# A list scheduler's cost model: transfers with shared rates and margins, and one more accumulating load

## The chip, the cores and the metric

The kernel runs on one core of one Trainium2 chip. The metric is the device time of one execution in microseconds (us). In this document PE is TensorE (matrix products; PEld is its loading of weights), DVE is VectorE, ACT is ScalarE, POOL is GpSimd and SP is SyncE. A load is a DMA transfer from the chip's main memory (HBM) into the on-chip buffer; an accumulating load adds what it brings to what lies there. Both run on 16 DMA engines; the plain ones are issued by SP, the accumulating ones by POOL.

## The reference

A decoder of two layers on 256 positions of width 1024, all in float32:

```python
for i in range(DEPTH):                      # two layers
    if i % 2 == 0:                          # layer 0: spatial gating in 12 groups
        h = x @ a_w_in[li]; u, v, q_mem = split(h)
        mix = gmlp_mixer(u, v, ...)
    else:                                   # layer 1: causal attention, 12 heads of 64
        h = x @ b_w_in[li]; q, k, v, q_mem = split(h)
        mix = moba_attention(q, k, v)       # 256 positions are one block: own block alone
    mem_out = memory_cross_attention(q_mem, mem, w_mem_kv[i])   # 4 heads, 256 memory tokens
    sub = concatenate([mix, mem_out]) @ w_mix_out[i]
    x = layer_norm(ALPHA * x + sub, ...)
    x = layer_norm(ALPHA * x + swiglu(x, w_ffn_in[i], w_ffn_out[i]), ...)

def swiglu(x, w_in, w_out):
    g, u = split(x @ w_in)                  # 1024 -> 2 x 2816
    return (silu(g) * u) @ w_out            # 2816 -> 1024
```

## The kernel before

**Products.** To keep float32 precision on the fast matmul path, every operand is split into a high and a low half (`split`: ACT copies the high half, DVE subtracts it to get the low one), and each product is three passes: high·high, high·low, low·high. So every weight that is loaded costs ACT and DVE a split; 1024 columns of it are one piece.

**Channel mixer.** Its 11 chunks of 256 channels are done as one plain chunk (`R`) and five pairs (`S`, chunks 1-2, 3-4, 5-6, 7-8, 9-10; `PLANS`). A pair computes a 2 x 2 block product with seven instead of eight block products, M1 to M7 (Strassen's way, in `product`). `OPERAND` names the weight blocks of each: M1 needs block 11, M5 needs 11 + 12, M2 needs 21, M6 needs 11 + 22, M3 needs 22, M7 needs 12 + 22, M4 needs 21 + 11, where a former sum stays in its buffer and is part of the next operand. The sums are made in three ways: by DVE (`raw_s<-raw_s,raw_s`), by an accumulating load out of main memory (`LOADED`, M7: `raw_s<-in_w` on POOL) or by an accumulating transfer between two buffers (`MOVED`, M4: `raw_s<-raw_s` on POOL). The results are gathered in X, Y and Z (PSUM tiles), from which ACT and DVE make m1 and m5; `sg` is the silu that m5 needs. PE transposes m1 and m5 (`tp`), the pieces are split again (`ht`), and the output products (`fo`) follow. A last letter f or g in a tile's name stands for layer 0 or 1. In layer 1's first pair the seven products are interleaved with the plain chunk and the second half of the LayerNorm, so that they come in the order M1, M2, M5, M6, M3, M7, M4 (`ffn_steps`).

**Order.** Nothing runs where it is written: `Plan` records all instructions of the program with their dependences and then orders them. TensorE keeps the order of the recording. For DVE, ACT, POOL and SP, `simulate` is a list scheduler: it steps through time with assumed costs (`Op.cost`: `hold` is how long an engine is taken, `lat` when the result can be used), gives each engine the instruction that can start first and, among those, the one that is due first (`late`, from `deadlines`), and keeps an engine free for a short while if a more urgent instruction is about to be ready. Instructions made with `either` (copies and scalings) go to ACT or DVE, whichever is chosen first. It also chooses the slot of each tile. Five sets of constants are tried (`TRIALS`), and the order with the least planned waiting of TensorE is issued. The engines then run in that order, each instruction waiting for its semaphores, so only the order and the slots come from the plan, not the times. Since ACT, DVE, POOL and SP run in order, one that waits holds up all that stand behind it.

**Transfers in the plan before.** One serial link:

```python
size = op.bytes * (2.1 if e == "gpsimd" else 1) / 437
link = max(link, t + 2300) + size
end = max(link, t + 7800 if e == "gpsimd" else 0) + 100
```

Weights come in units of 1 MB (128 x 2048) into six `raw` buffers (`RAW_BUFS`), and ten split pieces (`HALF_BUFS`) are kept. `Stream.make` makes the next piece: it loads ahead as far as buffers are free, forms the sum where there is one, and splits.

Of the kernel before, what the change touches and what calls it, by code (L numbers as in the profile page):

```python
# [46 lines left out]
OPERAND = {"M1": ("11", None), "M5": ("11", "12"), "M2": ("21", None), "M3": ("22", None),  # L47
           "M6": ("11", "22"), "M7": ("12", "22"), "M4": ("21", "11")}
LOADED = ("M7",)
MOVED = ("M4",)  # L50
TAGS = {"11": "gb", "21": "vbig"}

# [150 lines left out]
class Op:  # L203
# [13 lines left out]
    def cost(self):  # L217

        w = max([v.width() for v in self.writes + self.reads] or [1])
        e, n = self.engine, self.name  # L220
        if n == "dma_start":
            v = (self.writes or self.reads)[0]
            self.bytes = 4 * v.ap.ap[0][1] * v.width()
            self.hold, self.lat = (900 if e == "gpsimd" else 400), 0
        elif e == "tensor":
            w = self.args[2].width() if n == "matmul" else P
            f32 = n == "matmul" and self.args[2].root.dtype == F32
            self.hold = max(104, (w + 32) / 2.4) if not f32 else 0.85 * w
            self.lat = 200 + 0.37 * w if not f32 else self.hold + 270
        elif e == "vector":  # L230
            slow = n in ("tensor_scalar_mul", "tensor_scalar_add") or n == "tensor_copy"
            self.lat = 225 + 0.48 * w if n == "tensor_scalar_mul" and w > 8 else 150 + 1.042 * w
            self.hold = self.lat - 82
        elif e == "scalar":
            self.lat = 190 + 0.842 * w + (200 if "accum_out" in self.kw else 0)
            self.hold = self.lat - 100
        else:
            self.lat = self.hold = 700 + 2.5 * w if w < 8 else 250 + 2.0 * w


class Plan:
# [48 lines left out]
    def delay(self, a, b):  # L290

        if a.engine == b.engine and a.name != "dma_start":
            return a.hold
        if a.name == "dma_start":
            return 2300 + a.bytes / 400 if a.engine != "gpsimd" else 2300 + a.bytes / 180
        return a.lat + (50 if b.engine == "tensor" else 33)

    def deadlines(self):
        t = 4300
        for op in self.ops:  # L300
            if op.engine == "tensor":
                op.late = t
                t += op.hold
        for op in self.ops:
            for o in op.before.values():
                o.after.append(op)
        slots, last, follow = {}, {}, {}
        for op in self.ops:
            for b in op.roots:
                last[b] = op.n  # L310
        for op in self.ops:
            for b in op.roots:
                if b.tile is None and b.slot is None:
                    free = slots.setdefault(b.tag, [(0, i, None) for i in range(b.bufs)])
                    free.sort()
                    n, b.slot, was = free.pop(0)
                    if was:
                        follow[was] = op
            for b in op.roots:
                if last[b] == op.n and b.tile is None:  # L320
                    slots[b.tag].append((op.n, b.slot, b))
        for op in reversed(self.ops):
            late = [o.late - self.delay(op, o) for o in op.after if o.late is not None]
            late += [follow[b].late - self.delay(op, follow[b]) for b in op.roots if b in follow]
            if op.late is not None:
                late.append(op.late)
            op.late = min(late) if late else t
            if op.engine == "tensor":
                op.due = op.late

    def order(self):
        self.deadlines()
        best = None
        for trial in self.TRIALS:
            for op in self.ops:
                for b in op.roots:
                    b.slot, b.last, b.left = None, 0.0, 0
            for op in self.ops:
                for b in op.roots:
                    b.left += 1  # L340
            out, lost = self.simulate(*trial)
            self.trials.append(lost)
            if best is None or lost < best[0]:
                best = lost, [(op, op.opens, op.call, op.start, op.end, [b.slot for b in op.opens]) for op in out]
        for op, op.opens, op.call, op.start, op.end, slots in best[1]:
            for b, b.slot in zip(op.opens, slots):
                pass
        return [x[0] for x in best[1]]

    def simulate(self, slip, idle, margin):  # L350
# [2 lines left out]
        head = {e: 0 for e in by_late}  # L353
        gone = set()
        free = {e: 0.0 for e in self.ENGINES}
        busy = dict(free)
        waiting = {op.n: len(op.before) for op in self.ops}
        at = {op.n: 0.0 for op in self.ops}
        ready = {e: [] for e in self.ENGINES}
        tags = {}  # L360
        for op in self.ops:
            for b in op.roots:
                if b.tile is None:
                    t = tags.setdefault(b.tag, {"queue": [], "slots": [(0.0, i) for i in range(b.bufs)]})
                    if b not in t["queue"]:
                        t["queue"].append(b)
        pe = [op for op in self.ops if op.engine == "tensor"]
        ip = 0
        link = 0.0
        for op in self.ops:  # L370
            if not waiting[op.n]:
                for e in op.calls():
                    ready[e].append(op)
        out = []

        def opening(op):

            t0 = at[op.n]
            for b in op.roots:
                if b.slot is not None or b.tile is not None:  # L380
                    continue
                t = tags[b.tag]
                i = t["queue"].index(b)
                need = i + 1 if len(t["slots"]) > i else 0
                if not need:
                    return None
                fit = [x for x in t["slots"] if not b.whole or x[1] in whole]
                if not fit:
                    return None
                t0 = max(t0, min(fit)[0])  # L390
            return t0

        def hope(op, memo, depth):

            if op in memo:
                return memo[op]
            t = at[op.n]
            if waiting[op.n]:
                for o in op.before.values():
                    if o in gone:  # L400
                        continue
                    if o.engine == "tensor":
                        s = free["tensor"] + o.due - pe[ip].due
                    elif depth == 0 or o.name == "dma_start":
                        t = 1e12
                        break
                    else:
                        s = max(hope(o, memo, depth - 1), free[o.engine])
                    t = max(t, s + self.delay(o, op))
            memo[op] = t  # L410
            return t

        while len(out) < len(self.ops):
# [64 lines left out]
            for b in op.opens:  # L478
                q = tags[b.tag]
                q["queue"].remove(b)  # L480
                fit = [x for x in q["slots"] if x[0] <= t] if not b.whole else [x for x in q["slots"] if x[1] in whole]
                s = min([x for x in fit if x[1] not in whole] or fit) if b.psum else min(q["slots"])
                q["slots"].remove(s)
                b.slot = s[1]
            if e == "tensor" and (op.name == "transpose" or op.kw["start"]):
# [2 lines left out]
                if b.tag == "mm":  # L488
                    (whole.add if full else whole.discard)(b.slot)
            if op.name == "dma_start":  # L490
                size = op.bytes * (2.1 if e == "gpsimd" else 1) / 437
                link = max(link, t + 2300) + size
                end = max(link, t + 7800 if e == "gpsimd" else 0) + 100
            else:
                end = t + op.call.lat
            op.end = end
            out.append(op)
            for o in op.after:
                w = t + op.call.hold if o.engine == e and not o.other and op.name != "dma_start" else end + (50 if o.engine == "tensor" else 33)
                at[o.n] = max(at[o.n], w)  # L500
                waiting[o.n] -= 1
                if not waiting[o.n] and o.engine != "tensor":
                    for e2 in o.calls():
                        ready[e2].append(o)
            for b in op.roots:
                b.left -= 1
                b.last = max(b.last, end + 33)
                if not b.left and b.slot is not None:
                    tags[b.tag]["slots"].append((b.last, b.slot))
        return out, lost  # L510

    def emit(self):
# [10 lines left out]
class Stream:  # L523
# [17 lines left out]
    def parts(self, key):  # L541

        if len(key) == 2:
            return [key[0]]
        return [f"{key[0]}_{q}" for q in OPERAND[key[1]][:1 if key[1] in LOADED else 2] if q]

    def unit_ap(self, name):
        off, n = OFFS[name]
# [20 lines left out]
    def make(self):  # L569
# [9 lines left out]
            self.nc.gpsimd.dma_start(self.raw[parts[0]], self.raw[parts[1]], accum_op=ALU.add)  # L579
        elif len(parts) == 2 and key[-1] == 0:  # L580
            self.nc.vector.tensor_add(self.raw[parts[0]], self.raw[parts[0]], self.raw[parts[1]])
        if key[1] in LOADED and key[-1] == 0:
            a, b = (f"{key[0]}_{q}" for q in OPERAND[key[1]])
            self.nc.gpsimd.dma_start(self.raw[a], self.unit_ap(b), accum_op=ALU.add)
        hl = self.tile("spl", [P, 2, 1024], F32R, "spl", "spl_" + "_".join(map(str, key)), HALF_BUFS)
# [875 lines left out]
```

## Time and profile before

| | |
|---|---|
| median of 3 runs | 571.65 us (571.44 to 573.89) |
| the profiled execution | 569.85 us, span from first to last instruction 568.1 us |
| mean granted TensorE clock | 0.992 |
| busy: PE / PEld / DVE / ACT / POOL | 550.0 / 475.2 / 506.1 / 370.8 / 32.7 us |
| moved by DMA | 131.48 MB, mean 231 GB/s |
| issues of 1 MB loads into `raw_s` by SP, median to landing | 40, 7.6 us |
| accumulating loads (`raw_s<-in_w`) / transfers (`raw_s<-raw_s`) by POOL | 10 of each, 9.0 / 7.7 us |

The profile is one execution. A row of the timeline gives the start in us from the span's start, the length, the engine, the line, the operation, the tiles (output<-inputs), the shapes and the count, and in brackets how long the engine was idle before it and whose result ended that. All recorded instructions are issued at line 520, so they are told apart by the names of their tiles. A row of the stretches' table gives each engine's busy time with its number of instructions, in the order PE, PEld, DVE, ACT, POOL, then the granted clock, the busy share of the DMA engines, and GB/s.

### The profile page before, as it was taken

The numbers are of one execution on the slowest core, as the hardware profiler recorded it, in microseconds if no ns is written. First come the engines' busy times: TensorE is split into PE (matmuls) and PEld (weight loads), VectorE is DVE, ScalarE is ACT, GpSimd is POOL, SyncE is SP. The second block draws the span as 40 slices with busy tenths as digits, with TensorE's granted clock in tenths as the row PEclk, the third lists the DMA queues.
The fourth block names the chain that finished last, engine by engine and source line by source line (L and its number), as shares of the span: only waits on it lengthen the run. The fifth ranks groups of instructions, "written<-read, shape, count | busy, mean of one in ns | idle before, by whom it ended". The sixth has DMA issues, their size and how long they took to land. (4 is left out here: it accounts for less than half of the span.)

```text
span 568.1 us, 8070 instructions
## 1 busy us (share of the span) xinstructions
PE 550.0 (97%) x3028; PEld 475.2 (84%) x3028; DVE 506.1 (89%) x674; ACT 370.8 (65%) x563; POOL 32.7 (6%) x44
## 2 busy tenths in 40 slices
PE   8999999999999999999999999999989899999995
PEld 8999879878887888788899989888868688788884
DVE  5789989999989999996987898699999799899965
ACT  6767755696558594774476989566766575848710
POOL 2020000000000000100100000000000000001001
PEclk9999999999999999999999999999999999999998
DMA  8999744576796989799456253352777969797902
GB/s 293 381 379 387 301 177 154 144 213 203 197 377 167 377 215 364 205 346 352 167 186 260 74 186 149 77 172 85 236 219 198 356 171 374 177 359 214 288 1 75
DMA packets 23352, 131.48 MB, mean 231 GB/s; under 512 B 2576, under 2 KB 6288, under 8 KB 9360
## 3 DMA queue, kind: packets, MB, share of 16 engines
q1 hardware_dynamic: 20000, 109.45, 49.7%
q0 software_dynamic: 2880, 20.97, 19.6%
q8 instruction: 24, 0.39, 0.3%
q10 hardware_dynamic: 432, 0.52, 0.3%
q14 instruction: 16, 0.13, 0.1%
HBM read 119.41 MB, written 1.05 MB: 212 GB/s over the span
## 5 line engine op out<-in xcount | busy, mean ns | idle before, releaser
L520 ACT CAST spl_s_M<-raw_s 128x1024 fp32r<-128x1024 f32 x140 | 139.8, 1050 | 53.4 <-DMA raw_s<-in_w 25.1
L520 DVE TENSOR_TENSOR spl_s_M<-raw_s,spl_s_M 128x1024 fp32r<-128x1024 f32 x140 | 164.4, 1219 | 7.2 <-ACT spl_s_M L520 7.0
L520 PE MATMUL fog<-spl_w,htg 128*128 128x512 f32 (+1 forms) x282 | 64.9, 382 | 0.0
L520 PE MATMUL fof<-spl_w,htf 128*128 128x512 f32 x264 | 63.9, 392 | 0.0
L520 ACT CAST spl_w<-raw_w 128x1024 fp32r<-128x1024 f32 x44 | 45.7, 1052 | 27.0 <-DMA raw_w<-in_w 16.0
L520 PEld LDWEIGHTS fog<-spl_w,htg 128*128 128x128 f32 x282 | 51.0, 191 | 9.7
L520 PEld LDWEIGHTS fof<-spl_w,htf 128*128 128x128 f32 x264 | 49.0, 188 | 9.9
L520 DVE TENSOR_TENSOR spl_w<-raw_w,spl_w 128x1024 fp32r<-128x1024 f32 x44 | 53.2, 1218 | 0.4 <-ACT spl_w L520 0.4
L520 DVE TENSOR_TENSOR raw_s<-raw_s,raw_s 128x2048 f32<-128x2048 f32 x20 | 45.7, 2284 | 0.0
L520 PE MATMUL qk<-x2T,spl_qk 128*128 128x256 f32 x288 | 36.4, 284 | 1.2 <-DVE mix L520 1.2
L520 PEld LDWEIGHTS qk<-x2T,spl_qk 128*128 128x128 f32 x288 | 35.2, 192 | 1.4 <-DVE mix L520 1.4
L520 PE MATMUL Xf<-spl_s_M,x1T 128*128 128x512 f32 x120 | 28.4, 391 | 1.3 <-DVE m5f L520 1.2
L520 PE MATMUL Zg<-spl_s_M,SgM 128*128 128x512 f32 x120 | 29.0, 390 | 0.6 <-DVE htg L520 0.6
L520 PE MATMUL Zf<-spl_s_M,SfM 128*128 128x512 f32 x120 | 29.0, 390 | 0.0
L520 PE MATMUL Xg<-spl_s_M,SgM 128*128 128x512 f32 x120 | 29.0, 390 | 0.0
L520 PE MATMUL Xf<-spl_s_M,SfM 128*128 128x512 f32 x120 | 28.8, 389 | 0.0
L520 PE MATMUL Xg<-spl_s_M,x3T 128*128 128x512 f32 x120 | 28.4, 391 | 0.0
L520 PEld LDWEIGHTS Xf<-spl_s_M,x1T 128*128 128x128 f32 x120 | 22.4, 188 | 6.7 <-ACT spl_s_M L520 1.6
L520 PEld LDWEIGHTS Zg<-spl_s_M,SgM 128*128 128x128 f32 x120 | 22.5, 188 | 5.7 <-DVE htg L520 1.1
L520 PEld LDWEIGHTS Xg<-spl_s_M,x3T 128*128 128x128 f32 x120 | 22.4, 188 | 5.1 <-DVE m5g L520 0.3
L520 PEld LDWEIGHTS Xf<-spl_s_M,SfM 128*128 128x128 f32 x120 | 22.5, 188 | 4.7
L520 PEld LDWEIGHTS Xg<-spl_s_M,SgM 128*128 128x128 f32 x120 | 22.5, 188 | 4.6
(245 smaller groups left out, 1004.8 us busy)
## 6 DMA issues: line engine op xcount, KB each, us to landing
raw_s<-in_w SPq DMA_DIRECT2D x40, 1024.0 KB, 7.6
raw_w<-in_w SPq DMA_DIRECT2D x22, 1024.0 KB, 8.6
raw_s<-in_w POOLq DMA_DIRECT2D x10, 1024.0 KB, 9.0
raw_s<-raw_s POOLq DMA_DIRECT2D x10, 1024.0 KB, 7.7
raw_o<-in_w SPq DMA_DIRECT2D x8, 1024.0 KB, 6.3
raw_qk<-in_w SPq DMA_DIRECT2D x6, 1024.0 KB, 4.8
raw_u<-in_w SPq DMA_DIRECT2D x3, 1024.0 KB, 10.1
raw_bv<-in_w SPq DMA_DIRECT2D x4, 768.0 KB, 8.8
```

The lines of the kernel that those rows point to most:

```text
L520: getattr(getattr(self.nc, c.engine), c.name)(*map(real, c.args), **{k: real(v) for k, v in c.kw.items()})
```

## The change

Nothing in what is computed changes, and TensorE's order stays. Two things do.

The first is what the planner believes. `Op.cost` has new figures (a DVE operation on three operands 57 ns more, ACT's accumulating read shared out otherwise, POOL's short operations 985 ns, issues of DMAs 450 and 1000 ns instead of 400 and 900). A result used by the same engine is now ready after its latency, not after the engine's hold; POOL is taken to see a result 500 ns late. Transfers are modelled by a new class, `Wire`, with a queue for plain and one for accumulating transfers, a rate for each, lower rates when both run, at most eight of SP's transfers under way, and a margin (`SPARE`) behind the modelled end before data or a slot count as usable (`sure`).

The second is an operand: in layer 1's first pair (`s1_1`), M5's sum 11 + 12 is formed by an accumulating load of block 12 out of main memory, as M7's already was, and no longer by DVE. Block 12 is still loaded by itself too, for M7.

```diff
+FIRST_LOADED = {"s1_1": ("M5", "M7")}
...
-            self.hold, self.lat = (900 if e == "gpsimd" else 400), 0
+            self.hold, self.lat = (1000 if e == "gpsimd" else 450), 0
...
-            self.lat = 225 + 0.48 * w if n == "tensor_scalar_mul" and w > 8 else 150 + 1.042 * w
+            self.lat = 225 + 0.48 * w if fast else 152 + 1.042 * w
+            if n == "scalar_tensor_tensor" and not psum:
+                self.lat += 57
...
-            self.lat = 190 + 0.842 * w + (200 if "accum_out" in self.kw else 0)
-            self.hold = self.lat - 100
+            self.lat = 190 + 0.842 * w + (90 if "accum_out" in self.kw else 0) - (35 if psum else 0)
+            self.hold = self.lat - 98 + (100 if "accum_out" in self.kw else 0)
...
-            self.lat = self.hold = 700 + 2.5 * w if w < 8 else 250 + 2.0 * w
+            self.lat = self.hold = 985 if w < 8 else 300 + 1.4 * w
+
+class Wire:
+    HARD, SOFT, BOTH, LANES = ((7000, 250), (30000, 370), (1e12, 428)), 223, (155, 123), 8
+    SPARE = 1200, 1800
+
+    def __init__(self):
+        self.now, self.hard, self.soft, self.sent = 0.0, [], [], []
+
+    def lane(self):
+        return self.sent[-self.LANES].end + 30 if len(self.sent) >= self.LANES else 0.0
+
+    def issue(self, op, t):
+        self.run(t, [self.hard, self.soft])
+        if op.engine == "sync":
+            self.sent.append(op)
+        (self.soft if op.engine == "gpsimd" else self.hard).append([op, t + 2350, op.bytes])
+        self.run(1e12, [[list(x) for x in q] for q in (self.hard, self.soft)])
+
+    def run(self, until, queues):
+        hard, soft = queues
+        now = self.now
+        while (hard or soft) and now < until:
+            live = [bool(q) and q[0][1] <= now for q in queues]
+            edge, hard_rate = next(x for x in self.HARD if now < x[0])
+            rates = self.BOTH if all(live) else (hard_rate * live[0], self.SOFT * live[1])
+            ends = [now + q[0][2] / r for q, r, a in zip(queues, rates, live) if a]
+            stop = min(ends + [edge] + [q[0][1] for q, a in zip(queues, live) if q and not a] + [until])
+            for q, r, a in zip(queues, rates, live):
+                if a:
+                    q[0][2] -= (stop - now) * r
+                    if q[0][2] < 1:
+                        op = q.pop(0)[0]
+                        op.end = stop + 100
+                        op.sure = stop + (self.SPARE[op.engine == "gpsimd"] if stop > 20000 else 200)
+            now = stop
+        if until < 1e12:
+            self.now = until
...
-            return a.hold
+            return a.hold if a.engine == "tensor" else a.lat + 35
...
-        return a.lat + (50 if b.engine == "tensor" else 33)
+        return a.lat + {"tensor": 56, "gpsimd": 500}.get(b.engine, 35)
...
+        free["sync"] = 800.0
...
+        def free_at(x):
+            b = x[0]
+            return max([b.last] + [o.sure for o in b.moves]) if b else 0.0
...
-            t0 = at[op.n]
+            t0 = max([at[op.n]] + [o.sure for o in op.moves])
+            if op.engine == "sync":
+                t0 = max(t0, wire.lane())
...
-                t0 = max(t0, min(fit)[0])
+                t0 = max(t0, min(map(free_at, fit)))
...
-                size = op.bytes * (2.1 if e == "gpsimd" else 1) / 437
-                link = max(link, t + 2300) + size
-                end = max(link, t + 7800 if e == "gpsimd" else 0) + 100
+                wire.issue(op, t)
+                end = 0
...
-        return [f"{key[0]}_{q}" for q in OPERAND[key[1]][:1 if key[1] in LOADED else 2] if q]
+        return [f"{key[0]}_{q}" for q in OPERAND[key[1]][:1 if key[1] in FIRST_LOADED.get(key[0], LOADED) else 2] if q]
...
-        if key[1] in LOADED and key[-1] == 0:
+        if key[1] in FIRST_LOADED.get(key[0], LOADED) and key[-1] == 0:
```

More of the change, by code (lines that the diff above doesn't have):

```diff
@@ L220, in cost @@
         e, n = self.engine, self.name
+        psum = any(v.root.psum for v in self.writes + self.reads)
         if n == "dma_start":
@@ L228, in cost @@
             self.hold = max(104, (w + 32) / 2.4) if not f32 else 0.85 * w
-            self.lat = 200 + 0.37 * w if not f32 else self.hold + 270
+            self.lat = (205 + 0.36 * w if n == "matmul" else 273) if not f32 else self.hold + 280
         elif e == "vector":
-            slow = n in ("tensor_scalar_mul", "tensor_scalar_add") or n == "tensor_copy"
-            self.lat = 225 + 0.48 * w if n == "tensor_scalar_mul" and w > 8 else 150 + 1.042 * w
+            fast = n == "tensor_scalar_mul" and w > 8
@@ L304, in deadlines @@
         for op in self.ops:
+            op.moves = [o for o in op.before.values() if o.name == "dma_start"]
             for o in op.before.values():
@@ L336, in order @@
                 for b in op.roots:
-                    b.slot, b.last, b.left = None, 0.0, 0
+                    b.slot, b.last, b.left, b.moves = None, 0.0, 0, []
             for op in self.ops:
@@ L363, in simulate @@
                 if b.tile is None:
-                    t = tags.setdefault(b.tag, {"queue": [], "slots": [(0.0, i) for i in range(b.bufs)]})
+                    t = tags.setdefault(b.tag, {"queue": [], "slots": [(None, i) for i in range(b.bufs)]})
                     if b not in t["queue"]:
@@ L368, in simulate @@
         ip = 0
-        link = 0.0
+        wire = Wire()
         for op in self.ops:
@@ L396, in hope @@
                 return memo[op]
-            t = at[op.n]
+            t = max([at[op.n]] + [o.sure for o in op.moves if o in gone])
             if waiting[op.n]:
@@ L480, in simulate @@
                 q["queue"].remove(b)
-                fit = [x for x in q["slots"] if x[0] <= t] if not b.whole else [x for x in q["slots"] if x[1] in whole]
-                s = min([x for x in fit if x[1] not in whole] or fit) if b.psum else min(q["slots"])
+                fit = [(free_at(x), x[1], x) for x in q["slots"] if not b.whole or x[1] in whole]
+                if b.psum:
+                    fit = [x for x in fit if x[0] <= t and x[1] not in whole] or fit
+                s = min(fit, key=lambda x: x[:2])[2]
                 q["slots"].remove(s)
@@ L490, in simulate @@
             if op.name == "dma_start":
-                size = op.bytes * (2.1 if e == "gpsimd" else 1) / 437
-                link = max(link, t + 2300) + size
-                end = max(link, t + 7800 if e == "gpsimd" else 0) + 100
-            else:
-                end = t + op.call.lat
-            op.end = end
+                wire.issue(op, t)
+                end = 0
+            else:
+                op.end = end = t + op.call.lat
             out.append(op)
             for o in op.after:
-                w = t + op.call.hold if o.engine == e and not o.other and op.name != "dma_start" else end + (50 if o.engine == "tensor" else 33)
-                at[o.n] = max(at[o.n], w)
+                if op.name != "dma_start":
+                    same = o.engine == e == "tensor"
+                    at[o.n] = max(at[o.n], t + op.call.hold if same else end + {"tensor": 56, "gpsimd": 500}.get(o.engine, 35))
                 waiting[o.n] -= 1
@@ L506, in simulate @@
                 b.left -= 1
-                b.last = max(b.last, end + 33)
+                b.last = max(b.last, end + 35)
+                if op.name == "dma_start":
+                    b.moves.append(op)
                 if not b.left and b.slot is not None:
-                    tags[b.tag]["slots"].append((b.last, b.slot))
+                    tags[b.tag]["slots"].append((b, b.slot))
         return out, lost
```

## The prediction

> **What bounds the kernel now.** I read the busy shares first, then the idle time of TensorE in the timeline, because TensorE is busy nearly throughout and only its waits can be won.
>
> ```profile
> PE 550.0 (97%) x3028; PEld 475.2 (84%) x3028; DVE 506.1 (89%) x674; ACT 370.8 (65%) x563; POOL 32.7 (6%) x44
> ```
>
> The TensorE order is written by hand and does not change, so the first instruction after a wait names the wait. These are the timeline's rows of PE with a wait over 0.25 us behind the start phase (start, length, instruction, wait in brackets; the rows between them are left out), and the products that run just before the longest wait (445.83):
>
> ```profile
> 116.68 0.88 PE L520 MATMUL tpf<-ident,hf 128*128 128x128 f32 x4 [1.19 <-DVE hf L520]
> 171.78 0.33 PE L520 MATMUL tpf<-ident,m5f 128*128 128x128 f32 x1 [1.48 <-DVE m5f L520]
> 229.69 2.55 PE L520 MATMUL Xf<-spl_s_M,x1T 128*128 128x512 f32 x10 [1.19 <-DVE m5f L520]
> 336.14 2.06 PE L520 MATMUL qk<-x2T,spl_qk 128*128 128x256 f32 x15 [1.23 <-DVE mix L520]
> 418.87 0.33 PE L520 MATMUL tpg<-ident,m1g 128*128 128x128 f32 x1 [0.56 <-DVE m1g L520]
> 419.47 0.33 PE L520 MATMUL tpg<-ident,m5g 128*128 128x128 f32 x1 [0.27 <-DVE m5g L520]
> 423.86 3.03 PE L520 MATMUL Zg<-spl_s_M,SgM 128*128 128x512 f32 x12 [0.64 <-DVE htg L520]
> 445.83 5.70 PE L520 MATMUL Xg<-spl_s_M,x3T 128*128 128x512 f32 x24
> 453.63 0.44 PE L520 MATMUL tpg<-ident,m5g 128*128 128x128 f32 x1 [2.00 <-DVE m5g L520]
> 486.93 0.33 PE L520 MATMUL tpg<-ident,m5g 128*128 128x128 f32 x1 [0.64 <-DVE m5g L520]
> ```
>
> The waits are 9.20 us together. The stretches around the longest one show a further cost, in the clock column (after the engines' busy times):
>
> ```profile
> 450.00:453.60 3.60, 1.64 (x8) 1.08 (x6) 0.93 (x3) 3.23 (x4) 0.06 (x1) 1.00 1.05 225
> 453.60:457.10 3.50, 3.46 (x12) 3.08 (x13) 3.50 (x4) 3.50 (x6) 0.00 (x0) 0.52 1.02 264
> ```
>
> After the wait of 2.00 us the granted clock was 0.52 for 3.5 us; 0.48 of 3.5 is 1.68 us lost. So 10.9 us is the most that a better order can win behind the start. Every one of these waits names DVE, but why was DVE late? At 453 us the chain of waits, then ACT and DVE, say it:
>
> ```profile
> 439.50 10.76 DMA raw_s<-in_w
> ```
> ```profile
> 447.89 1.05 ACT L520 CAST spl_w<-raw_w 128x1024 fp32r<-128x1024 f32 x1 [4.25 <-DMA raw_w<-in_w]
> 450.37 1.99 ACT L520 CAST spl_s_M<-raw_s 128x1024 fp32r<-128x1024 f32 x2 [1.43 <-DMA raw_s<-in_w]
> 452.26 0.59 ACT L520 ACTIVATE sgg<-Xg 128x512 f32<-128x512 f32 x1
> ```
> ```profile
> 452.89 0.69 DVE L520 SCALAR_TENSOR_TENSOR m5g<-m5g,sgg 128x512 f32<-128x512 f32 x1 [2.67 <-ACT sgg L520]
> ```
>
> ACT, in order, stood before a load that landed at 450.26 and then split it twice, with the short silu (sgg) behind that; DVE sat idle 2.67 us for sgg, and TensorE waited for DVE. The planner had put the split first; below I work out why. Over the whole run ACT waited 25.1 us, 15 times, for such loads:
>
> ```profile
> ACT spl_s_M L520 <- DMA raw_s<-in_w: 25.1, 15, 3.9
> ```
> ```profile
> DMA to landing us min/median/max: 4.7/8.0/11.9
> ```
>
> The last row is for all transfers into raw_s. The old cost of a 1 MB load is 2.3 us plus 2.4 us on one serial link, 4.7 us: the minimum of that row, not its median of 8.0.
>
> **The change, part by part.**
>
> *Costs and transfers in the planner (Op.cost, Wire, opening, free_at).* No instruction of the chip gets longer or shorter; what changes is the order on DVE, ACT, POOL and SP, which of DVE and ACT makes each copy, and which buffer slot is taken. Every issue of SP may move; one takes 0.33 us (the row of 439.07 below). I go through the waits and ask what the new costs do to the decision behind each.
>
> At 453 us the decision can be worked out. The accumulating load was issued at 431.19, and SP loads at:
>
> ```profile
> 435.15 1.64 SPq L520 DMA_DIRECT2D raw_s<-in_w  x2
> 439.07 0.33 SPq L520 DMA_DIRECT2D raw_w<-in_w  x1
> 439.50 3.40 SPq L520 DMA_DIRECT2D raw_s<-in_w  x2
> ```
> ```profile
> 431.19 0.85 POOL L520 DMA_DIRECT2D raw_s<-raw_s  x1 [11.46 <-ACT spl_s_M L520]
> ```
>
> Old formula: link to 431.19 + 2.3 + 5.04 = 438.5, then four loads of 2.4 us, so the load of 439.50 ends at 448.2; on the chip it landed 2.1 us later. New formula: the accumulating load runs alone at 223 B/ns from 433.5, beside the first plain one from 437.5 to 438.8, and then 428 B/ns: 448.2 again, but usable only 1.2 us later by the margin, 449.4. ACT is free of spl_w's split at 448.8, and sgg can start when the product M4 is done at about 448.9 (the middle of 24 matmuls begun at 445.83). So the old costs put the split first, the new ones sgg; m5g would be ready near 450.2, before TensorE asks at 451.6. The wait goes, and with it the slow clock: 2.00 + 1.68 = 3.68 us. What is late next is the split, by 0.5 us.
>
> The waits at 486.93 and 423.86 have the same form: ACT waited for a load, made a train of splits, and the short operation came behind them (sgg, and htg at 422.5).
>
> ```profile
> 481.77 3.90 ACT L520 CAST spl_s_M<-raw_s 128x1024 fp32r<-128x1024 f32 x4 [1.42 <-DMA raw_s<-in_w]
> 485.57 0.58 ACT L520 ACTIVATE sgg<-Xg 128x512 f32<-128x512 f32 x1
> ```
> ```profile
> 419.65 2.95 ACT L520 CAST spl_s_M<-raw_s 128x1024 fp32r<-128x1024 f32 x3 [1.31 <-DMA raw_s<-in_w]
> ```
>
> Two times 0.64: 1.28 us more. Transfers explain 4.96 us in all, and I take all of it.
>
> The waits at 171.78, 229.69 and 336.14 (3.90 us) are orders too, but no plain matter of transfers: a long split or sum went ahead of the short operation that TensorE needed, as here,
>
> ```profile
> 167.56 2.95 ACT L520 CAST spl_s_M<-raw_s 128x1024 fp32r<-128x1024 f32 x3 [1.43 <-PE Xf L520]
> 170.42 0.58 ACT L520 ACTIVATE sgf<-Xf 128x512 f32<-128x512 f32 x1
> ```
>
> where all four became ready with the same TensorE event. The new engine costs differ by 60 ns at most for such operations, so only the reshuffle can help; ends 0 and 3.90, I take half, 1.95 us.
>
> The waits at 116.68 and 418.87/419.47 (1.19 + 0.83) I leave standing, because there DVE had no room:
>
> ```profile
> 95.00:115.00 20.00, 20.00 (x117) 17.72 (x117) 19.02 (x23) 12.86 (x21) 1.79 (x2) 1.00 0.57 159
> ```
> ```profile
> 385.00:415.00 30.00, 30.00 (x140) 24.76 (x139) 29.96 (x36) 19.84 (x27) 1.31 (x2) 1.00 0.57 179
> ```
>
> (third pair of numbers: DVE 19.02 of 20 and 29.96 of 30 us). Against all this, a new order makes new waits. The nearest price is the present order's own mean, 9.20/9 = 1.0 us each; ends 0 and nine of them. I take one: most present waits are bought by the error that is corrected.
>
> *The M5 operand of layer 1's first pair.* It removes one DVE sum of 2.28 us and adds one accumulating load of 1 MB with its POOL issue; unit 12 is read from memory twice.
>
> ```profile
> 361.70 2.29 DVE L520 TENSOR_TENSOR raw_s<-raw_s,raw_s 128x2048 f32<-128x2048 f32 x1
> 366.46 0.42 DVE L520 TENSOR_TENSOR mix<-pv,mix 128x256 fp32r<-128x256 f32 x1 [2.47 <-ACT mix L520]
> ```
> ```profile
> 364.64 0.88 POOL L520 DMA_DIRECT2D raw_s<-in_w  x1 [81.62 <-DVE raw_s L520]
> 374.90 0.99 POOL L520 TENSOR_TENSOR rsc<-rsc,mhalf 128x1 f32<-128x1 f32 x1 [9.38 <-DVE rsc L520]
> ```
> The sum stood before 2.47 us of DVE idleness, so its removal is worth nothing there; at most it moves work ahead of the full stretch from 385, 0.83 us (the two waits left standing). The new load waits on POOL for M1's two splits, which end on DVE near 358.6; behind it stand M7's load and the LayerNorm powers, the first at 374.90, with POOL idle before. Even with the longest landing, 11.9 us, it is there by 358.6 + 0.9 + 11.9 = 371.4, and M5's splits start on ACT at 380.76. No loss, then; I take 0. If M7's load goes out behind it, its landing is still ahead of its use near 400.
>
> *Sum*: 4.96 + 1.95 − 1.0 = 5.9 us. The profiled execution took 569.85 us for its span of 568.1; it lies 1.8 us under the median of the runs, 571.65. So 564.0 on the profile's scale, 565.75 on the median's.
>
> On the clock: by the row above a wait of 2.00 us was followed by the slow clock, while 1.48 us at 171.78 was not. The Trainium skill ("TensorE: Matmul & The Clock Gate", What's actually happening) has the half rate come after at least one idle window of about 3.4 us. By that rule the 2.00 us would not be the cause, and 1.68 us would stay; the slow stretch's length of 3.5 us agrees with the page's window, the length of the wait before it does not.
>
> **The rivals.**
>
> *A: no room on DVE.* If DVE is what the layers run at, waits removed come back elsewhere.
>
> ```profile
> 115.00:262.00 147.00, 143.05 (x647) 117.42 (x646) 141.67 (x138) 101.64 (x122) 7.07 (x9) 1.00 0.86 274
> ```
> ```profile
> 385.00:513.00 128.00, 123.90 (x553) 101.37 (x552) 121.54 (x119) 83.27 (x102) 6.44 (x8) 0.99 0.78 246
> ```
>
> Without 1.48, twice 1.19 us the first would hold 141.67 us of DVE in 143.1, 99%; the second 121.54 in 122.2 without its 5.8, over 99%. For it: these sums. Against it: part of that work is ahead of need, and DVE was idle 2.67 us just before the longest wait. If both stretches keep their DVE shares, only the wait at 336.14 goes: 571.65 − 1.23 = 570.4.
>
> *B: slower, the margins put splits too late.* The planner now thinks a load unusable 1.2 us (accumulating ones 1.8 us) past its modelled end, and gives ACT and DVE other work first; where the load was there in time, the next product's split stands behind another job. The nearest price is one split of DVE:
>
> ```profile
> L520 DVE TENSOR_TENSOR spl_s_M<-raw_s,spl_s_M 128x1024 fp32r<-128x1024 f32 x140 | 164.4, 1219 | 7.2 <-ACT spl_s_M L520 7.0
> ```
>
> 164.4/140 = 1.17 us. One such wait in each of ten pairs is 11.7 us: 571.65 − 5.9 + 11.7 = 577.4. It undoes the gain from six pairs on, and is slower beyond half a per cent from eight. For it: DVE's full stretches, where each late job is paid. Against it: the median landing of 8.0 us lies above even 4.8 + 1.2, so the margin is mostly real.
>
> *C: all waits go*, those of the full DVE stretches too, because work is taken ahead: 571.65 − 10.9 = 560.8. Against it are DVE's 29.96 of 30 us.
>
> *D: the slow clock stays* though the wait goes: 565.75 + 1.68 = 567.4. For it only that waits of 1.48 and 2.00 us behaved differently, and one instance is thin. It is also what the skill's rule, above, would give.
>
> **How the numbers follow.** Forecast 0.55, A 0.20, B 0.12, C 0.08, D 0.05. Half a per cent, 2.9 us, is about what a measurement of this kernel can tell from no change. Faster (under 568.8): 0.55 + 0.08 + 0.05 = 0.68; within: A, 0.20; slower (over 574.5): 0.12. The likeliest case has its own range from 562.8 (8.86 us, all but the full stretches) to 568.7. The range for all reaches from 560.7 (C) to 573.5 (A with three new waits of 1.0 us), and leaves B out.
>
> **What would show it.** sgg ahead of the splits and no 2 us wait of TensorE in layer 1, the granted clock at 1.00 there; ACT's waits on raw_s loads well under 25 us; the M5 load issued on POOL near 359 and one DVE sum less (19). Against me: as many TensorE waits as now at other places with DVE full before them (A), waits of products on splits whose load had long landed (B), or a slow clock without a wait before it (D).

## The result, and the profile after

The changed kernel takes 563.23 us (median of 4 runs, 563.13 to 563.66) against 571.91 us (571.44 to 573.89) of the kernel before on the same chip: a ratio of 0.9843, with a 95% interval from 0.9819 to 0.9867. That is 8.7 us less by the medians. Between the two profiled executions it is 6.7 us: 569.85 us before, 563.18 us after, for a span of 561.5 us. The profile of before was one of its quicker runs; after, all runs lie within 0.6 us.

The busy shares of the changed kernel:

```profile
PE 548.5 (98%) x3028; PEld 473.2 (84%) x3028; DVE 503.4 (90%) x673; ACT 370.0 (66%) x563; POOL 33.7 (6%) x45
```

One DVE instruction less, and on POOL one DMA issue more; the work is the same to within 3 us on every engine. What went is idle time of TensorE. Its timeline now has these rows with a wait behind the start phase:

```profile
116.13 0.88 PE L574 MATMUL tpf<-ident,hf 128*128 128x128 f32 x4 [0.71 <-DVE hf L574]
...
174.10 3.02 PE L574 MATMUL Zf<-spl_s_M,SfM 128*128 128x512 f32 x12 [0.26 <-DVE htf L574]
...
232.80 0.33 PE L574 MATMUL tpf<-ident,m5f 128*128 128x128 f32 x1 [0.27 <-DVE m5f L574]
...
264.50 0.66 PE L574 MATMUL tpf<-ident,m5f 128*128 128x128 f32 x4 [0.21 <-DVE m5f L574]
...
333.48 3.13 PE L574 MATMUL qk<-x2T,spl_qk 128*128 128x256 f32 x24 [0.76 <-DVE mix L574]
...
399.68 0.79 PE L574 MATMUL tpg<-ident,hg 128*128 128x128 f32 x4 [0.26 <-DVE hg L574]
401.66 2.56 PE L574 MATMUL Xg<-spl_s_M,SgM 128*128 128x512 f32 x10 [0.72 <-DVE SgM L574]
...
418.28 0.33 PE L574 MATMUL tpg<-ident,m1g 128*128 128x128 f32 x1 [0.46 <-DVE m1g L574]
418.88 0.33 PE L574 MATMUL tpg<-ident,m5g 128*128 128x128 f32 x1 [0.28 <-DVE m5g L574]
```

They are 3.9 us together; before they were 9.2. In layer 1 there is none behind the first pair, and no slow clock: the long stretch of that layer has 1.00 in the clock column. With the 1.68 us of the slow stretch, 5.3 + 1.7 = 7.0 us went, which is the 6.7 us between the two profiles within 0.3 us.

```profile
385.00:513.00 128.00, 126.28 (x576) 103.73 (x575) 123.79 (x121) 87.88 (x107) 6.90 (x8) 1.00 0.82 260
```

The decision that the prediction worked through at 453 us of the kernel before is the same place at 447 us here. ACT and DVE:

```profile
445.75 1.05 ACT L574 CAST spl_w<-raw_w 128x1024 fp32r<-128x1024 f32 x1 [4.08 <-DMA raw_w<-in_w]
447.13 0.60 ACT L574 ACTIVATE sgg<-Xg 128x512 f32<-128x512 f32 x1 [0.32 <-PE Xg L574]
448.23 2.95 ACT L574 CAST spl_s_M<-raw_s 128x1024 fp32r<-128x1024 f32 x3 [0.50 <-DMA raw_s<-in_w]
```
```profile
447.76 0.69 DVE L574 SCALAR_TENSOR_TENSOR m5g<-m5g,sgg 128x512 f32<-128x512 f32 x1
```

The silu runs ahead of the splits, m5g is done at 448.4, and TensorE, which needs it at 449.8, never stops. Look at the first and the third row: the split of the load starts 2.48 us after the split of the load before it, exactly as before (447.89 and 450.37). The transfers did not get faster. For all transfers into raw_s the landing has the same median to 0.2 us, and a longer maximum:

```profile
DMA to landing us min/median/max: 4.7/7.8/12.6
```

### The profile page after: what moved, and what is told of

It is laid out like the page before. It is cut to its first block, busy times and chain, and to the rows that moved or that the text cites. A ratio compares the mean times of both kernels' runs of the same rounds, so it can differ in the third digit from the quotient of the medians.

```text
span 561.5 us, 8058 instructions
## 1 busy us (share of the span) xinstructions
PE 548.5 (98%) x3028; PEld 473.2 (84%) x3028; DVE 503.4 (90%) x673; ACT 370.0 (66%) x563; POOL 33.7 (6%) x45
## 4 chain that ended last, share of the span: by engine, by line
PE 61%; DVE 18%; DMA 9%; ACT 6%; issue 4%; SPq 0%; DVEq 0%; ACTq 0%; POOLq 0%
PE fog L574 10%; PE Xg L574 7%; DVE spl_s_M L574 6%; DMA raw_s<-in_w 4%; PE opa L574 4%; PE Zg L574 4%; PE qk L574 4%; PE fof L574 3%; PE pu L574 3%; PE bv L574 3%; PE Xf L574 3%; DMA raw_s<-raw_s 3%; DVE raw_s L574 3%; PE opc L574 2%; PE va L574 2%
## 5 line engine op out<-in xcount | busy, mean ns | idle before, releaser
L574 DVE TENSOR_TENSOR raw_s<-raw_s,raw_s 128x2048 f32<-128x2048 f32 x19 | 43.5, 2292 | 0.0
L574 PEld LDWEIGHTS Zf<-spl_s_M,SfM 128*128 128x128 f32 x120 | 22.3, 188 | 5.6 <-DVE htf L574 1.0
```

The lines of the kernel that those rows point to most:

```text
L574: getattr(getattr(self.nc, c.engine), c.name)(*map(real, c.args), **{k: real(v) for k, v in c.kw.items()})
```

## The experiments

The theory to test (T) was that the gain is what the planner believes of transfers, and that the operand and the engine costs are worth little. Its rivals: the operand (M), the engine costs (E), and luck (L), since a list scheduler moves some hundred instructions at any touch.

All ratios are to runs of the kernel before beside them on the same chip (its medians there: 570.69 to 571.91 us). "Waits on m5" are TensorE's waits for m5 (in the rows of tp, X), added up from each kernel's profile; the wait worked through at 453 us is one of them.

| kernel | transfers | margin, us plain/acc. | engine costs | M5 loaded | median us | ratio (95%) | waits on m5, us |
|---|---|---|---|---|---|---|---|
| before | link | none | old | no | 571.91 | 1 | 5.6 |
| after | Wire | 1.2 / 1.8 | new | yes | 563.23 | 0.9843 (0.9819 to 0.9867) | 0.8 |
| e1 | Wire | 1.2 / 1.8 | new | no | 566.42 | 0.9922 (0.9892 to 0.9953) | 0.7 |
| e2 | link | none | old | yes | 573.75 | 1.0046 (1.0024 to 1.0069) | 7.0 |
| e3 | link | none | new | yes | 566.85 | 0.9922 (0.9892 to 0.9952) | 5.0 |
| e4 | Wire | 1.2 / 1.8 | old | yes | 562.27 | 0.9846 (0.9812 to 0.9879) | 0.3 |
| e5 | Wire | none | new | yes | 570.60 | 0.9984 (0.9962 to 1.0006) | 6.7 |
| e6 | Wire | 2.4 / 3.6 | new | yes | 562.87 | 0.9849 (0.9816 to 0.9882) | 0.3 |
| e7 | link | none | old, nudged | no | 572.81 | 1.0015 (0.9995 to 1.0035) | 7.6 |
| e8 | link | none | old, own latency | no | 571.10 | 0.9991 (0.9972 to 1.0011) | 7.6 |
| e9 | Wire | 0 / 1.8 | new | yes | 567.59 | 0.9942 (0.9922 to 0.9962) | 4.1 |
| e10 | Wire | 1.2 / 0 | new | yes | 563.09 | 0.9851 (0.9818 to 0.9884) | 0.4 |
| e11 | link | 1.2 / 1.8 | old | no | 566.55 | 0.9908 (0.9878 to 0.9938) | 4.2 |
| e12 | Wire | 2.4 / 3.6 | old, own latency | yes | 562.45 | 0.9841 (0.9808 to 0.9873) | 0.3 |

### The parts apart: e1 to e4

e1, from the changed kernel:

```diff
-FIRST_LOADED = {"s1_1": ("M5", "M7")}
+FIRST_LOADED = {}
```

> The changed kernel with M5's sum in layer 1's first pair back on DVE. Theory T (the gain is the transfer model; the operand is worth nothing where it stood): 563.2 us, within 1.5. Rival M (the sum taken off DVE eases the full stretch behind it): 565 us or more, with longer waits at 415 to 424. Rival L (any reshuffle moves the time by some us, the order is luck): anywhere from 560 to 570.

It was 566.42 us, so T's "worth nothing" is wrong, and so is M's place for it: the waits at 415 to 424 stayed as they are. The new wait is elsewhere, in TensorE's and DVE's timelines of e1:

```profile
360.66 1.19 PE L574 MATMUL pt<-ident,pb 128*128 128x128 f32 x6 [1.89 <-DVE pb L574]
```
```profile
356.02 2.28 DVE L574 TENSOR_TENSOR raw_s<-raw_s,raw_s 128x2048 f32<-128x2048 f32 x1
358.22 0.42 DVE L574 CUSTOM_DVE_ANT_0 pb<-s,mask 128x256 f32<-128x256 f32 x1
```

The sum of M5 now runs 2.28 us right ahead of the last softmax of the attention, and TensorE waits 1.89 us for its result. In the changed kernel that softmax starts on DVE at 356.86, behind a copy of 0.55 us instead of the sum, and the wait is gone; its POOL rows show the two loads of M5 and M7 out early, with nothing queued behind them for 15 us:

```profile
356.40 0.55 DVE L574 COPY pT<-pt 128x384 f32<-128x384 f32 x1
356.86 0.42 DVE L574 CUSTOM_DVE_ANT_0 pb<-s,mask 128x256 f32<-128x256 f32 x1
```
```profile
353.08 0.88 POOL L574 DMA_DIRECT2D raw_s<-in_w  x1 [71.48 <-DVE spl_s_M L574]
356.56 0.88 POOL L574 DMA_DIRECT2D raw_s<-in_w  x1 [2.61 <-DVE mix L574]
```

e1 is a close comparison: going by the tiles' names, the orders of the two kernels on DVE, ACT, POOL and SP differ in nothing but this sum, the load that takes its place, and two copies (pT<-pt).

e2, from the kernel before: the same operand alone (`FIRST_LOADED` and its two uses in `Stream`).

> The kernel before with nothing but M5's operand by an accumulating load. T: 571.9 us, within 1.5. M: 569 us or less. L: anywhere from 565 to 578.

It was slower, by 0.24 to 0.69%. The waits on m5 are 7.0 us instead of 5.6, in pairs of both layers: a reshuffle far from the operand. By itself the operand gains nothing.

e3, from the changed kernel: `Wire` holds the old formula.

```diff
+    def lane(self):
+        return 0.0
+    def issue(self, op, t):
+        soft = op.engine == "gpsimd"
+        self.link = max(self.link, t + 2300) + op.bytes * (2.1 if soft else 1) / 437
+        op.end = max(self.link, t + 7800 if soft else 0) + 100
+        op.sure = op.end + 33
```

> The changed kernel with the old serial link in place of Wire (no shared rates, no lanes, no margin), but all new engine costs and the M5 operand. T: about 570 us, the slow clock stretch or waits over 1.5 us of TensorE in layer 1 back, ACT's waits on raw_s loads at 25 us again. Rival E (the engine costs, above all that a result is ready for its own engine only after its latency, are what helps): about 564 us. L: no telling.

It lies between T and E: 566.85 us, with 5.0 us of waits on m5. ACT's waits on raw_s loads are back, as T had it (27.5 us), but no wait of TensorE in layer 1 is over 1.00 us and no stretch is slow. e4 is the other half, `Op.cost`, `delay` and the readiness of results as before, the rest as changed.

> The changed kernel with Wire, its margins and the M5 operand, but the old engine costs and the old readiness of results for the same engine. T: 563 to 566 us, no wait of TensorE over 1.5 us in layer 1. E: about 571 us. L: no telling.

It is as fast as the changed kernel, and the pairs of layer 0 and those of layer 1 behind the first have no wait that the timeline shows. So the engine costs are not needed, as T has it, and E falls. That e3 was nonetheless faster than before is followed up below.

### Which part of Wire: e5, e6, e9, e10, e11

Each of the first four is one line, as here e5:

```diff
-    SPARE = 1200, 1800
+    SPARE = 0, 0
```

> The changed kernel with no margin behind a transfer's modelled end (SPARE = 0, 0). Theory Margin (the order is robust because data count as late): waits of TensorE on m5 of 0.5 us and more come back in the pairs, about 566 us. Rival Rates (the shared rates alone put the transfers right): 563 us, within 1.

> The changed kernel with twice the margins (2400 and 3600 ns). Theory Margin: what there is to win is won, 563 us, within 1. Rival B of the prediction (splits put behind other work while their data lie there): 565 us or more, TensorE waiting for splits whose load has landed.

Without the margins the gain is gone, though rates, lanes, engine costs and operand are all there. The loss is larger than I had expected (566 us). The new rates and lanes alone show no gain: e5 is even slower than e3, which has the old link in their place (ratios 0.9984 and 0.9922). ACT of e5 at the place of the worked decision:

```profile
450.31 1.06 ACT L574 CAST spl_w<-raw_w 128x1024 fp32r<-128x1024 f32 x1 [4.09 <-DMA raw_w<-in_w]
452.80 1.05 ACT L574 CAST spl_s_M<-raw_s 128x1024 fp32r<-128x1024 f32 x1 [1.43 <-DVE spl_w L574]
453.76 0.58 ACT L574 ACTIVATE sgg<-Xg 128x512 f32<-128x512 f32 x1
```

The split is ahead of the silu again, and TensorE waits for m5g. (The row at 452.80 names DVE, whose own split ended just then; the 2.49 us from split to split are the step of the landings.)

```profile
455.12 0.33 PE L574 MATMUL tpg<-ident,m5g 128*128 128x128 f32 x1 [0.98 <-DVE m5g L574]
```

Twice the margins change nothing, and that refutes rival B of the prediction: thinking a load late costs nothing here even at 2.4 and 3.6 us. Which margin it is:

> The changed kernel with a margin behind accumulating transfers alone (SPARE = 0, 1800). Theory Soft (it is the accumulating transfers, above all M4's, that held up ACT: its wait on raw_s<-raw_s fell from 11.4 us without margins to 3.2 with them): 563 to 564 us. Theory Hard (the plain loads' margin does it): 568 to 571 us, waits of TensorE on m5 near 1 us in every pair. Theory Both (each removes its share): about 567 us.

> The changed kernel with a margin behind plain loads alone (SPARE = 1200, 0). Soft: 568 to 571 us. Hard: 563 to 564 us. Both: about 567 us.

Hard is right: 1.2 us behind plain loads alone give all of it. I had leaned to Soft, because ACT's waits for raw_s<-raw_s had fallen most. In e10 they are where they were without margins, and it is as fast as the changed kernel:

```profile
ACT spl_s_M L574 <- DMA raw_s<-in_w: 20.1, 12, 3.9
ACT spl_s_M L574 <- DMA raw_s<-raw_s: 11.9, 6, 3.1
```

How long ACT waits for loads is not what matters; what stands behind the wait is. The margin behind accumulating transfers gives a part (e9, 0.58%), through the slots that they free or by another order; the runs do not tell which.

e11 puts the margins into the kernel before, as one line behind `end`:

```diff
+                end += 0 if end < 20000 else 1800 if e == "gpsimd" else 1200
```

> The kernel before with one line more: the old serial link, and 1200 ns (plain) or 1800 ns (accumulating) behind its end. No new rates, no new engine costs, M5's sum on DVE. Theory Margin (the margin is the change): 564 to 567 us, the waits on m5 in the pairs gone. Rival (a margin is only worth something behind the right rates): 569 us or more. Rival L: anywhere, with waits on m5 still there.

One line gives 0.92% (0.62 to 1.22) of the 1.57%. I had expected the waits on m5 to be gone; they are 4.2 us, none over 1.4 us, and without a slow stretch. It is level with e1, the other kernel with margins whose M5 sum is on DVE, so beside the margins e1's rates, lanes and engine costs show no gain either. The old link with margins and the M5 load together was not run.

### Luck, and the own latency: e7 and e8

e7 sets 50 to 56 and 33 to 35 in the hand-over times of the kernel before; e8 leaves them as they were (its expectation calls it nudged, but the constants stay at 50 and 33) and lets a result be ready for its own engine only after its latency:

```diff
-            return a.hold
+            return a.hold if a.engine == "tensor" else a.lat + 33
...
-                w = t + op.call.hold if o.engine == e and not o.other and op.name != "dma_start" else end + (...)
+                w = t + op.call.hold if o.engine == e == "tensor" else end + (...)
```

> The kernel before with its three hand-over constants 2 to 6 ns larger (50 to 56, 33 to 35): it corrects nothing worth naming, but reorders some hundred instructions. It measures luck. Theory T (the gain is in what the planner believes of transfers): 571.3 us, within 1.5, and waits on m5 in layer 1 as before. Rival L (any reshuffle moves the time by several us): under 568 or over 575.

> The kernel before, nudged as e7, and with a result ready for its own engine only after its latency (the one engine cost that differs by more than 60 ns; it shifts each dependent step by 115 ns). Theory E (this is what made the old link with the new engine costs fast): about 567 us. Theory T: 571 us, within 1.5. Rival L: as for e7.

Both times stay within 0.35% of the kernel before, and the waits on m5 stay. So these two touches alone do not make the gain, and the own latency does not explain e3. It does remove one wait: that for hf near 116 us is 1.19 to 1.21 us in before, e2, e4, e7 and e11, and 0.70 to 0.76 us in every kernel with the own latency. What made e3 faster than e2 is not settled: another of its costs (issue times of DMAs, POOL's 500 ns) or its order.

A touch can still be worth something: e2 lost 0.5% and e3 won 0.8%, both without a margin. What speaks against luck is that five kernels with the plain margin and the M5 load (after, e4, e6, e10, e12) lie between 0.9841 and 0.9851, though going by the tiles' names any two of them have at least 140 of some 1420 instructions of DVE, ACT, POOL and SP in another place.

### An attempt at a better one: e12

Twice the margins, the old costs of TensorE, DVE, ACT and POOL, the own latency, the new issue and hand-over times.

> An attempt at a better version: the changed kernel with twice the margins, the old engine costs for DVE, ACT and POOL, and results for the same engine ready after their latency. If the waits that are left in the pairs go as they did with the old costs (none there) and the start is that of the kernel before (0.7 us of waits): 561.5 us. If the old costs bring back the start's waits of 2 us: 563 us.

The pairs have hardly a wait left, but the start has 1.5 us and a transposition at 388 us a new one of 0.89 us. 562.45 us is not told apart from the changed kernel, nor are e4, e6 and e10. No run beat it clearly.

## Why the prediction was right, and where it was not

I forecast 565.7 us and faster; 563.2 us was measured.

*The mechanism* was right. The step worked out at 453 us held in each part: the old and the new rates give the same end there (448.2), only the margin puts sgg first. e5, without margins, has the split first; the changed kernel and e10 do not wait there.

*The transfers' term, 4.96 us:* the waits of 2.00, 0.64 and 0.64 us and the slow stretch are all gone. Right.

*The term for 171.78, 229.69 and 336.14, half of 3.90 us:* too small. The wait at 171.78 was misread. I called it no plain matter of transfers, since the row at 167.56 named a TensorE event as what ended ACT's wait. ACT's row ahead of it in the kernel before shows more:

```profile
165.09 1.05 ACT L520 CAST spl_w<-raw_w 128x1024 fp32r<-128x1024 f32 x1 [4.17 <-DMA raw_w<-in_w]
```

From 165.09 to 167.56 it is 2.47 us, the step of one load landing behind another, as from 447.89 to 450.37, so ACT most likely waited for a load. ACT at this place in e5 and in the changed kernel:

```profile
167.83 2.00 ACT L574 CAST spl_s_M<-raw_s 128x1024 fp32r<-128x1024 f32 x2 [1.42 <-DMA raw_s<-in_w]
169.73 0.59 ACT L574 ACTIVATE sgf<-Xf 128x512 f32<-128x512 f32 x1
```
```profile
167.78 1.05 ACT L574 CAST spl_s_M<-raw_s 128x1024 fp32r<-128x1024 f32 x1 [1.43 <-DMA raw_s<-in_w]
168.73 0.59 ACT L574 ACTIVATE sgf<-Xf 128x512 f32<-128x512 f32 x1
```

Three splits ahead of the silu before, two without margins, one with them; TensorE's wait behind it was 1.48, 1.15 and nothing. At 229.69 the reading was right: DVE had no idle time there, its sum stood ahead of the short operation that TensorE needed.

```profile
226.66 2.28 DVE L520 TENSOR_TENSOR raw_s<-raw_s,raw_s 128x2048 f32<-128x2048 f32 x1
228.86 0.68 DVE L520 TENSOR_TENSOR m5f<-m5f,Xf 128x512 f32<-128x512 f32 x1
```

In the changed kernel the short one comes first (225.25, the sum at 226.45) and the wait is gone; e5 has 0.81 us there, but e9, without the plain margin, has none, so what turned this order is not shown. Of 336.14, 0.76 of 1.23 us stayed. That part is no matter of margins: it is 0.75 to 0.77 us in e3, e5, e6, e9 and e10, all with the new engine costs, and 1.21 to 1.43 us in e2, e4, e7, e8, e11 and e12. Of the 3.90 us about 3.1 went, not 1.95.

*Waits left standing, 1.19 and 0.83 us:* 0.71 and 0.74 us stand. The first fell with the own latency (e8), which I had not priced.

*One new wait of 1.0 us:* the waits at 399.68 and 401.66 are 0.98 us; three of 0.21 to 0.27 come on top, 1.7 us in all.

*The M5 operand, 0 us:* wrong. The step took DVE's idle time behind the sum at 361.70 as cover, and that cover belonged to the old order. In the new one the sum comes ahead of the softmax and costs 1.89 us of waiting (e1); the ratios of after and e1 differ by 0.8%, some 4.5 us. Between the two profiled runs it is 1.96 us (563.18 and 565.14), about this wait; what makes the rest between the medians is open.

*The sum* on the profile's scale: 5.9 us forecast, 6.7 us measured. That it is this near is in part luck: two terms were too small (the three waits by 1.2 us, those left standing by 0.6), the new waits 0.7 us more than I took, and the operand's 0 us hid a wait that the new order has without it.

*Profile and median:* I carried the profile's offset of 1.8 us over to the median. It shrank to 0.1 us, for the changed kernel's runs lie together, so 2 us of the 8.7 are this.

*Rival A* (no room on DVE) fell: DVE's share of 385 to 513 rose from 121.54 to 123.79 of 128 us, with more of TensorE's instructions in the same stretch (553 before, 576 after). *B* fell with e6. *C* did not come: 3.9 us of waits are left. *D* did not come: with the wait of 2.00 us the slow stretch went too. Of the signs I named, ACT's waits on raw_s loads fell as I had said (25.1 to 12.2 us), but the gain does not need it: in e10 they are 20.1 us.

## What to carry to other kernels

An engine that works its queue in order is held up by an operation on data that are late, so an order planned ahead should not count transfers as early as the model of a link has them. Twice the margin cost nothing measurable here; leaving out the 1.2 us behind plain loads, with landings at a median of 8.0 us, cost 1.3% (e10 against e5). Whether the margin covers the scatter of the landings or a model that is too early on the mean, the runs do not tell: at 453 us of the kernel before the load came 2.1 us behind both models' end, later than the margin of 1.2 us reaches. To find such places, look not at how long an engine waits for transfers but at the short operation right behind the wait and at who needs it.

## What the hardware showed that I had not expected

*The slow clock does not go by the wait's length alone.* e7 has two waits of TensorE over 2 us; its timeline, and the stretches of 3.5 us behind each:

```profile
454.23 0.33 PE L520 MATMUL tpg<-ident,m5g 128*128 128x128 f32 x1 [2.11 <-DVE m5g L520]
487.74 0.33 PE L520 MATMUL tpg<-ident,m5g 128*128 128x128 f32 x1 [2.44 <-DVE m5g L520]
```
```profile
454.20:457.70 3.50, 3.47 (x19) 2.99 (x20) 3.50 (x4) 3.50 (x6) 0.00 (x0) 1.00 0.97 250
487.90:491.40 3.50, 3.50 (x13) 3.01 (x13) 2.44 (x3) 3.37 (x5) 0.00 (x0) 0.51 0.91 300
```

2.11 us left the clock at 1.00, 2.44 us was followed by 0.51, and in the kernel before 2.00 us was enough for 0.52. In e2 even 1.88 us was (at 455.89, clock 0.62 in the 3.5 us from 455.80 and 0.90 in the next), while 1.89 us in e1 left it at 1.00. The Trainium skill ("TensorE: Matmul & The Clock Gate", What's actually happening) has the activity watched in windows of 3413 ns that run freely and do not start anew with the kernel, and the half rate come after at least one idle window. That a longer wait can pass where a shorter one does not agrees with free windows; that a whole window must be idle does not agree with slow stretches behind waits of 1.9 to 2.4 us. In these kernels a wait near 2 us cost 1.7 us more in some places and nothing in others.

*Some orders with margins also scatter less.* The changed kernel, e6, e10 and e12 each lie within 0.9 us (4 runs each); the kernel before spread over 2.5 us in 4 runs and 5.6 us in 25, e5 over 4.1 us in 10. It is no rule: e4 and e1, with margins too, spread over 2.4 and 2.1 us (4 and 5 runs), e7, without, over 2.2 us in 10. e4's slowest run is the profiled one, where a wait of 2.02 us in the start phase was followed by a clock of 0.56. That the loads' scatter in landing no longer reaches TensorE may be the reason; no run took it apart.
